# Down projection of a hybrid decoder layer: 18 of 22 contraction tiles in the seven-product block form

## The chip, the cores and the metric

The kernel runs on one core of a Trainium2 chip. The metric is device time in microseconds (us) for one launch, as the median of several runs. The engines go by their short names: PE is TensorE, DVE is VectorE, ACT is ScalarE, POOL is GpSimd, SP is SyncE, which issues nearly all DMA transfers of this kernel.

## The reference

One inference step of a decoder layer, for a prompt of 1024 tokens and 8 sample tokens, which share all weights: 1032 token columns in all. Two mixers (a gated linear recurrence and a state-space mixer) are followed by an output projection, and then by the part that matters here:

```python
x = x + jnp.concatenate([o_a, y], axis=-1) @ w['w_out']
h = rmsnorm(x, w['norm2_w'])
gate, val = jnp.split(h @ w['w_up'], 2, axis=-1)              # 1024 -> 2 x 2816
gate, buf_f_new = causal_dwconv(gate, buf_f, w['ffn_conv_w'], w['ffn_conv_b'])   # width 3
x = x + (jax.nn.silu(gate) * val) @ w['w_down']               # 2816 -> 1024
...
y = rmsnorm(x, final_norm_w)
```

All of it is float32. A matrix product is made of three passes over operands that are split into a high part (rounded to the fp32r format) and a low part (the rest): high×high, high×low, low×high.

## The kernel before

Data lie transposed: 128 features on the partitions, 1032 tokens along the free axis. `DFF` = 2816 makes 22 feature tiles (`FT`), the model width 1024 makes 8 (`KT`). The tokens are split into four blocks of 258 (`QW`).

**Up projection, seven-product form.** A step j makes one feature tile of the gate and one of the value for all tokens. Both are products of a 2×2 block problem: two output tiles (gate, value), two halves of the contraction (4 tiles each), two token blocks. Instead of eight block products it takes seven, p1 to p7, of sums and differences of the operands. The weight sums are made on POOL from two staged tiles `ws` (`up_load`), and split into high `wh` and low `wl` by ACT and DVE (`up_split`). The token operands (`usets`) are made once before the stage. A step runs the products in `ORDER` = p1, p6, p5, p7, p2, p4, p3, each for both halves of the tokens (i = 0, 1), 12 matmuls a product, 168 in all. The results of one product are folded into the others by methods named after the products: some on ACT (copies of p1 and p5), some on DVE (adds that read PSUM), two POOL subtractions after p7. p1, p7 and p3 use three PSUM banks in turn (`ua`), the others four (`ub`). `up_close` then runs the convolution (`fcv`, one ACT and two DVE operations over 1048 columns), SiLU on ACT, the product with the value on DVE, and stores the activation tile in device memory (`act_d`).

**What sets the order.** The PE order is written out by hand: the loops issue matmuls one by one, and other work is tied to them with `tick()` and `after(n, ...)` (do it n matmuls later) and `spread(pieces, n)` (a piece of a generator every n matmuls). The order of the other engines' queues comes from a scheduler of the framework, which keeps to dependences; each queue then runs strictly in order. The staging tile `ws` has two buffers; the load of the next weights waits on SP until DVE has made the last split that reads the old ones.

**Down projection.** Five rounds of four contraction tiles (`RND`), and then a last stage of two tiles. In a round the four activation tiles are loaded from `act_d` and split (`act_load`); for each pair of output tiles 512 KB of weights are loaded and split (`wload`), and `down` runs 12 matmuls for each of 8 output tiles and 4 token quarters. DVE adds the PSUM result to the residual tile `xT`. The last stage takes its two tiles with resident weights (`wd`), quarter by quarter, in the order 3, 0, 1, 2; behind each quarter the final norm and the stores of the output (`fin`, `ot`) follow.

Names of tiles that appear below: `ub`, `ua`, `dn` are PSUM results; `ws`, `wt` staged weights and their sums; `wh`, `wl` their high and low parts; `us` intermediate blocks of an up step; `wdh`, `wdl` the plain weights of the last stage; `ah`, `al` plain activations. Line 93 is the one place that issues a matmul.

Of the kernel before, what the change touches and what calls it, by code (L numbers as in the profile page):

```python
# [16 lines left out]
P = 128  # L17
# [16 lines left out]
RND = 4  # L34
NRES = 4
# [8 lines left out]
        "x5": (UW, 5), "us": (QW, 10), "t": (512, 4)}  # L44
# [6 lines left out]
def hybrid_layer(  # L51
# [1124 lines left out]

    def up_load(j):
        ws = []
        for c0 in (0, DFF):
# [4 lines left out]
            last_w[0] = SP.dma_start(t.rearrange("p (k m) -> p k m", m=P),  # L1184
                                     w_up[0, :, c0 + j * P:c0 + (j + 1) * P].rearrange("(k p) m -> p k m", p=P))
            ws.append(t)
        (g1, g2), (v1, v2) = ((t[:, :512], t[:, 512:]) for t in ws)
        sums = {}

        def add(name, x_, y_):  # L1190
            sums[name] = tl("t", "wt")
            G.tensor_tensor(sums[name], x_, y_, op=ALU.add)
            return sums[name]
# [8 lines left out]
    def up_split(j, n):  # L1202
# [4 lines left out]
        lo = pool.tile([P, KT * P], F32R, tag="wl", bufs=2, name=nm("wl"))  # L1207
        for i, name in enumerate(ORDER[2 * n:2 * n + 2]):
            cs = slice(i * 512, (i + 1) * 512)
# [4 lines left out]
    class Up:  # L1214

        def __init__(self, j, i, ext, val):
            self.j, self.i, self.ext, self.val = j, i, ext, val

        def mul(self, name):
            w, u = wparts[self.j][1][name], usets[self.i][name]  # L1220
            ps = (psmm.tile([P, 512], F32, tag="mm", name=nm("ua")) if name in ("p1", "p7", "p3") else bank("ub"))[:, :QW]
            for k in range(4):
                for n, (a, x) in enumerate(((w[0], u[0]), (w[0], u[1]), (w[1], u[0]))):
                    mm(ps, a[:, k, :], x[:, k, :], start=k == 0 and n == 0, stop=k == 3 and n == 2)
# [3 lines left out]
        def at(self, c):  # L1228
            return slice((2 * self.i + c) * QW, (2 * self.i + c + 1) * QW)

# [33 lines left out]

    def up_open(j):
# [16 lines left out]
    def ups(j, seq):  # L1282

        us_ = up_open(j)
        for n, (name, i) in enumerate(seq):
            yield from us_[i].mul(name)
            if n == 2 and j + 1 < FT:
                up_load(j + 1)
            if n in (5, 9, 13) and j + 1 < FT:
# [3 lines left out]
        up_close(j, us_[0])  # L1293

    with tc.manual_schedule(engines={mybir.EngineType.PE}):
# [18 lines left out]

        xT = [None] * KT
        quarters = [slice(0, 256), slice(256, 512), slice(512, 768), slice(768, NT)]

        def act_load(k):
            hi, lo = tl("hT", "ah", F32R), tl("hT", "al", F32R)
            SP.dma_start(lo.bitcast(F32), act_d[k])  # L1320
            split_in(hi, lo, slice(0, NT))
            return hi, lo
# [14 lines left out]

        after(200, lambda: spread(ffn_conv_states(), 60))

        def down(w, kt, msl, acts, c):  # L1340
            q = quarters[c]
            ps = psmm.tile([P, 512], F32, tag="mm", name=nm("dn"))[:, :q.stop - q.start]
            for k in range(kt):
                hi, lo = acts[k]
                wh, wl = w(k)
                mm(ps, wh[:, msl], hi[:, q], start=(k == 0), stop=False)
                mm(ps, wh[:, msl], lo[:, q], start=False, stop=False)
                mm(ps, wl[:, msl], hi[:, q], start=False, stop=(k == kt - 1))
                tick()
            return ps  # L1350

        acts = [act_load(k) for k in range(RND)]
        for r0 in range(0, FT - RND, RND):
            nk = min(RND, FT - r0)
            rows = slice(r0 * P, (r0 + nk) * P)
            nxt = [act_load(r0 + RND + k) for k in range(min(RND, FT - r0 - RND))]
            for m in range(0, KT, 2):
                wh, wl = wload(w_down[0, rows, m * P:(m + 2) * P], nk, 2 * P)
                for i in range(2):
                    if xT[m + i] is None:  # L1360
# [74 lines left out]
```

## Time and profile before

| what | value |
|---|---|
| median of 3 runs | 1800.01 us (1798.77 to 1801.22) |
| profiled execution, its time | 1797.69 us |
| its span, first to last instruction | 1795.8 us |
| granted TensorE clock, mean | 0.987 |
| busy: PE, DVE, ACT, POOL | 97%, 63%, 44%, 23% |
| DMA moved | 182.34 MB, mean 102 GB/s |

In the rows of the profile `L1211` is line 1211 of the kernel, `x44` counts instructions, `out<-in` names tiles with their buffer numbers left out. A row of the groups gives busy time and mean duration, and then the engine's idle time before these instructions with what ended it. A row of the stretches gives the stretch, its length, the busy time of PE, the weight loads, DVE, ACT and POOL in it with their instruction counts, the granted clock, the mean busy share of the 16 DMA engines and GB/s. A row of the timeline gives start, duration, engine, line and operation. A row of the chain of waits gives start, duration and what ran. A row of the waits gives who waited for whom, us in total, how often, and the longest.

### The profile page before, as it was taken

To read this page: it belongs to the slowest core of one execution; us is meant where nothing else is said; L and a number is where in the kernel's file an instruction comes from. 1 tells how busy PE (TensorE), PEld (TensorE's weight loads), DVE (VectorE), ACT (ScalarE), POOL (GpSimd) and SP (SyncE) were. 2 spreads that over 40 slices of the span, in tenths; PEclk is the share of its full clock that TensorE was granted. 3 is DMA by queue.
4 is the path that set the end of the run, shared out by engine and by line. 5 is a ranking of instruction groups with operands and counts; after the bars stand their busy time and mean duration, and the time that the engine had idled before them with its cause. 6 is when DMAs were issued, how large, how long until landed. Compare 5 with 4: busy or idle time off the path is not lost.

```text
span 1795.8 us, 38458 instructions
## 1 busy us (share of the span) xinstructions
PE 1735.7 (97%) x16143; PEld 1680.2 (94%) x16143; DVE 1126.4 (63%) x2011; ACT 792.8 (44%) x1416; POOL 409.5 (23%) x415
## 2 busy tenths in 40 slices
PE   7999899999999999999999988999999999999998
PEld 6998799998999999999899977999999999999997
DVE  6667966565554555557636779656666667555545
ACT  7677688353444344345323344333433334111114
POOL 2113322110110110111100454445444542000001
PEclk9999999999999999999999988999999999999999
DMA  4144634642221222234334431222222225422212
GB/s 153 39 125 135 193 96 124 186 132 97 73 78 50 84 74 73 62 96 148 93 123 130 138 95 45 94 75 72 76 85 89 72 71 201 149 89 96 96 60 95
DMA packets 218019, 182.34 MB, mean 102 GB/s; under 512 B 13388, under 2 KB 195158, under 8 KB 217830
## 3 DMA queue, kind: packets, MB, share of 16 engines
q1 hardware_dynamic: 217558, 179.80, 32.0%
q8 instruction: 126, 2.06, 0.5%
q14 instruction: 47, 0.39, 0.1%
q0 software_dynamic: 288, 0.10, 0.0%
HBM read 141.53 MB, written 38.52 MB: 100 GB/s over the span
## 4 chain that ended last, share of the span: by engine, by line
PE 78%; DVE 7%; DMA 5%; ACT 4%; issue 3%; POOL 2%; SPq 1%; DVEq 0%; POOLq 0%; ACTq 0%
PE mm L93 31%; PE ub L93 14%; PE dn L93 13%; PE ua L93 10%; PE a L93 2%; PE o L93 1%; DMA csb<-cs_d 1%; DMA Bb<-bc_d 1%; ACT csb L530 1%; PE kv L93 1%; DVE wl L184 1%; POOL Cb L631 1%; SPq L175 1%; DMA ml<-mix_d 1%; ACT L531 1%
## 5 line engine op out<-in xcount | busy, mean ns | idle before, releaser
L93 PE MATMUL mm<-hh,wh 128*128 128x344 f32 x1248 | 407.9, 327 | 0.0
L93 PE MATMUL mm<-hl,wh 128*128 128x344 f32 x1248 | 406.2, 326 | 0.0
L93 PE MATMUL mm<-hh,wl 128*128 128x344 f32 x1248 | 404.3, 324 | 0.0
L93 PEld LDWEIGHTS mm<-hh,wh 128*128 128x128 f32 x1248 | 236.2, 190 | 3.5 <-issue 0.9
L93 PEld LDWEIGHTS mm<-hl,wh 128*128 128x128 f32 x1248 | 236.1, 189 | 2.6 <-issue 0.9
L93 PEld LDWEIGHTS mm<-hh,wl 128*128 128x128 f32 x1248 | 236.4, 189 | 2.3 <-issue 1.0
L183 ACT CAST wh<-ws 128x1024 fp32r<-128x1024 f32 x96 | 100.5, 1047 | 259.5 <-PE dn L93 133.6
L93 PE MATMUL ub<-uh,wh 128*128 128x258 f32 x704 | 200.2, 284 | 7.8 <-ACT uh L1129 7.8
L93 PE MATMUL ub<-ul,wh 128*128 128x258 f32 x704 | 199.5, 283 | 0.8 <-DVE ul L1130 0.8
L93 PE MATMUL ub<-uh,wl 128*128 128x258 f32 x704 | 199.4, 283 | 0.0
L93 PE MATMUL dn<-ah,wh 128*128 128x256 f32 (+1 forms) x640 | 181.2, 283 | 1.2 <-DVE x L1365 1.2
L93 PE MATMUL dn<-al,wh 128*128 128x256 f32 (+1 forms) x640 | 180.6, 282 | 0.0
L93 PE MATMUL dn<-ah,wl 128*128 128x256 f32 (+1 forms) x640 | 180.1, 281 | 0.0
L93 PE MATMUL mm<-mh,wh 128*128 128x258 f32 x512 | 149.1, 291 | 10.7 <-DVE x L1026 10.7
L184 DVE TENSOR_TENSOR wl<-ws,wh 128x1024 fp32r<-128x1024 f32 x96 | 127.0, 1323 | 50.0 <-ACT wh L183 47.3
L93 PE MATMUL ua<-uh,wh 128*128 128x258 f32 x528 | 149.5, 283 | 0.0
L93 PE MATMUL ua<-ul,wh 128*128 128x258 f32 x528 | 149.1, 282 | 0.0
L93 PE MATMUL ua<-uh,wl 128*128 128x258 f32 x528 | 148.9, 282 | 0.0
L93 PE MATMUL mm<-ml,wh 128*128 128x258 f32 x512 | 147.7, 289 | 0.3 <-DVE ml L985 0.3
L93 PE MATMUL mm<-mh,wl 128*128 128x258 f32 x512 | 147.4, 288 | 0.0
L93 PEld LDWEIGHTS ub<-uh,wh 128*128 128x128 f32 x704 | 133.8, 190 | 8.1 <-ACT uh L1129 8.1
L93 PEld LDWEIGHTS ub<-ul,wh 128*128 128x128 f32 x704 | 134.3, 191 | 1.1 <-DVE ul L1130 1.1
(333 smaller groups left out, 3920.5 us busy)
## 6 DMA issues: line engine op xcount, KB each, us to landing
ws<-in_w_in_dram SPq DMA_DIRECT2D x52, 512.0 KB
ws<-in_w_up_dram SPq DMA_DIRECT2D x44, 512.0 KB
ws<-in_w_out_dram SPq DMA_DIRECT2D x24, 512.0 KB
act_d<-val SPq DMA_DIRECT2D x22, 516.0 KB
al<-act_d SPq DMA_DIRECT2D x22, 516.0 KB
ws<-in_w_down_dram SPq DMA_DIRECT2D x22, 512.0 KB
ml<-mix_d SPq DMA_DIRECT2D x48, 172.0 KB
csb<-cs_d SPq DMA_DIRECT2D x32, 256.0 KB
```

The source lines that it names most:

```text
L93: PE.matmul(out, lhsT, rhs, start=start, stop=stop)
L175: SP.dma_start(dst, src)
L183: A.copy(wh[:, :n], ws[:, :n])
L184: V.tensor_tensor(wl[:, :n], ws[:, :n], wh[:, :n].bitcast(F32), op=ALU.subtract)
L530: A.activation(csb3[:, h, :], csb3[:, h, :], AF.Relu, scale=-1.0, bias=cst[:, h0 + h:h0 + h + 1])
L531: A.activation(csb, csb, AF.Exp, scale=-1.0)
L631: G.tensor_tensor(Cb, Sd, Cb, op=ALU.mult)
```

## The change

Eighteen of the 22 contraction tiles of the down projection go into the seven-product form; four stay plain, in the last stage (`DPLAIN` = 4, two before). There are three rounds (`NRD`) of three pairs of contraction tiles (`RP`). A Down step j ≥ 22 belongs to round r and output pair q (`divmod(j - FT, 4)`), twelve steps in all, written (r,q) below. The 2×2 block problem is: two output tiles, two contraction tiles of a pair, two token blocks of 258; the three pairs of a round are summed in PSUM, so that a product takes 9 matmuls and a step 126.

The code of the up step is shared: `Seven.mul` runs a product, `Up` and `Down` differ in operands and in what happens to a result. In a Down step DVE adds p2, p4 and p3 straight to the residual tiles, with two further adds from SBUF for each half of the tokens, and POOL does four operations for each half.

The token operands of a pair need sums of two activation tiles, so they are made during the up projection, by `act_set`: after every odd step up to 17 it loads four blocks of the two finished activation tiles, makes four differences and sums on POOL, splits seven operands into high and low (`put`: ACT copy, DVE subtraction, 258 columns each), and stores them in device memory (`as_d`), for i = 0 and i = 1, one piece every 21 matmuls. In the down projection a round needs 21 tiles of 1032 columns (seven operands of three pairs, high and low of one half of the tokens side by side, both halves). They are loaded into buffers that the up projection leaves (`slot`); a list of loads (`wanted`) is worked off as buffers come free: the first round's during the last up step, the next round's first five during the step before the last of a round, the rest in the round's last step, each when a product is done. The loads and splits of the plain tiles (`last_tiles`) stand at the end of the same list.

```diff
-RND = 4
+RP, NRD = 3, 3
+DPLAIN = FT - 2 * RP * NRD
+    NSTEP = FT + 4 * NRD
     def up_load(j):
...
+            else:
+                r, q = divmod(j - FT, 4)
+                rows = w_down[0, 2 * RP * r * P:2 * RP * (r + 1) * P, (2 * q + i) * P:(2 * q + i + 1) * P]
+                for h2 in range(2):
+                    last_w[0] = SP.dma_start(t[:, h2 * n * P:(h2 + 1) * n * P].rearrange("p (k m) -> p k m", m=P),
+                                             rows.rearrange("(k two p) m -> two p k m", two=2, p=P)[h2])
...
+    class Down(Seven):
+        def operands(self, name):
+            return [[t[:, self.i, a, :] for t in dset[self.r, name]] for a in range(2)]
+        def p1(self, ps):
+            self.s = tl("us", "us")
+            A.copy(self.s, ps)
+        def p6(self, ps):
+            self.u2 = tl("us", "us")
+            V.tensor_tensor(self.u2, self.s, ps, op=ALU.add)
+        def p5(self, ps):
+            self.f = tl("us", "us")
+            A.copy(self.f, ps)
+            x_ = self.xg[:, self.at(0)]
+            G.tensor_tensor(x_, x_, self.s, op=ALU.add)
+        def p7(self, ps):
+            self.u3 = tl("us", "us")
+            V.tensor_tensor(self.u3, self.u2, ps, op=ALU.add)
+            G.tensor_tensor(self.u2, self.f, self.u2, op=ALU.subtract)
+            G.tensor_tensor(self.f, self.f, self.u3, op=ALU.subtract)
+            x_ = self.xv[:, self.at(1)]
+            G.tensor_tensor(x_, x_, self.f, op=ALU.add)
...
+        def p4(self, ps):
+            x_ = self.xg[:, self.at(1)]
+            V.tensor_tensor(x_, x_, ps, op=ALU.add)
+            V.tensor_tensor(x_, x_, self.u3, op=ALU.add)
...
+    def act_set(kp):
+        for i in range(2):
+            ab = tl("g", "ab")
+            for h2 in range(2):
+                SP.dma_start(ab[:, h2 * 2 * QW:(h2 + 1) * 2 * QW], act_d[2 * kp + h2][:, 2 * i * QW:2 * (i + 1) * QW])
+            yield
+            a1, b1, a2, b2 = (ab[:, n * QW:(n + 1) * QW] for n in range(4))
+            def put(name, src):
+                hl = tl("as", "as", F32R)
+                A.copy(hl[:, :QW], src)
+                V.tensor_tensor(hl[:, QW:], src, hl[:, :QW].bitcast(F32), op=ALU.subtract)
+                SP.dma_start(as_d[kp, ORDER.index(name)][:, 2 * i * QW:2 * (i + 1) * QW], hl.bitcast(F32))
+            put("p4", b2)
+            G.tensor_tensor(b2, b1, b2, op=ALU.subtract)
+            yield
+            put("p1", a1)
+            G.tensor_tensor(b1, a1, b1, op=ALU.subtract)
...
+    def wanted():
+        for r in range(NRD):
+            for name in ORDER:
+                for n in range(RP):
+                    while not free or r and turned[0] < (r - 1, 2):
+                        yield None
+                    yield lambda r=r, name=name, n=n: dset_load(r, name, n)
+        yield from last_tiles()
...
-        up_close(j, us_[0])
+            if i:
+                turn(j, name)
+        if j < FT:
+            up_close(j, us_[0])
+            if j % 2 and j < 2 * RP * NRD:
+                after(20, lambda: spread(act_set(j // 2), 21))
...
-        for r0 in range(0, FT - RND, RND):
...
+        for j in range(FT, NSTEP):
+            for _ in ups(j, [(name, i) for name in ORDER for i in range(2)]):
+                tick()
```

The PE order is unchanged up to the last up step. DVE's queue in the middle of an up step before: evictions of p7 (L1245), splits of two weights (L1211), evictions of p2 (L1251) and p4 (L1256).

```order
L1245 TENSOR_TENSOR us_17420<-us_17342,ua_17407 128x258
L1245 TENSOR_TENSOR us_17437<-us_17369,ua_17424 128x258
L1211 TENSOR_TENSOR wl_17470<-wt_17352,wh_17469 128x512
L1211 TENSOR_TENSOR wl_17470<-wt_17348,wh_17469 128x512
L1251 TENSOR_TENSOR fext_17291<-us_17308,ub_17441 128x258
L1251 TENSOR_TENSOR fext_17291<-us_17323,ub_17455 128x258
L1256 TENSOR_TENSOR fext_17291<-us_17420,ub_17475 128x258
L1256 TENSOR_TENSOR fext_17291<-us_17437,ub_17489 128x250
```

The same place now (p7 is L1265, the splits L1225, p2 L1271, p4 L1276; L1348 is the subtraction of `put`, from the block tile `ab`):

```order
L1265 TENSOR_TENSOR us_17743<-us_17650,ua_17725 128x258
L1265 TENSOR_TENSOR us_17760<-us_17682,ua_17747 128x258
L1225 TENSOR_TENSOR wl_17798<-wt_17660,wh_17797 128x512
L1348 TENSOR_TENSOR as_17670<-ab_17624,as_17670 128x258
L1348 TENSOR_TENSOR as_17702<-ab_17624,as_17702 128x258
L1271 TENSOR_TENSOR fext_17596<-us_17613,ub_17764 128x258
L1225 TENSOR_TENSOR wl_17798<-wt_17656,wh_17797 128x512
L1271 TENSOR_TENSOR fext_17596<-us_17631,ub_17783 128x258
L1276 TENSOR_TENSOR fext_17596<-us_17743,ub_17803 128x258
L1348 TENSOR_TENSOR as_17737<-ab_17624,as_17737 128x258
L1348 TENSOR_TENSOR as_17773<-ab_17624,as_17773 128x258
L1276 TENSOR_TENSOR fext_17596<-us_17760,ub_17821 128x250
```

Four of a step's seven new subtractions stand between the splits and the evictions of p2 and p4; the other three follow among the evictions of p3 and the convolution. POOL's queue over one up step before holds the four weight sums (L1192) and the four subtractions after p7 (L1246, L1247):

```order
L1192 TENSOR_TENSOR wt_17348<-ws_17346 128x512
L1192 TENSOR_TENSOR wt_17350<-wt_17348,ws_17344 128x512
L1192 TENSOR_TENSOR wt_17352<-ws_17344,ws_17346 128x512
L1192 TENSOR_TENSOR wt_17354<-wt_17350,ws_17344 128x512
L1246 TENSOR_TENSOR val_17292<-us_17384,us_17420 128x258
L1247 TENSOR_TENSOR us_17342<-us_17384,us_17342 128x258
L1246 TENSOR_TENSOR val_17292<-us_17399,us_17437 128x258
L1247 TENSOR_TENSOR us_17369<-us_17399,us_17369 128x258
L1267 MEMSET fext_17547 128x2
```

Now (sums L1205, the subtractions after p7 L1266 and L1267), the four block operations of `act_set` stand between them and the next step:

```order
L1205 TENSOR_TENSOR wt_17660<-ws_17652,ws_17654 128x512
L1205 TENSOR_TENSOR wt_17662<-wt_17658,ws_17652 128x512
L1266 TENSOR_TENSOR val_17597<-us_17697,us_17743 128x258
L1267 TENSOR_TENSOR us_17650<-us_17697,us_17650 128x258
L1266 TENSOR_TENSOR val_17597<-us_17717,us_17760 128x258
L1267 TENSOR_TENSOR us_17682<-us_17717,us_17682 128x258
L1352 TENSOR_TENSOR ab_17624<-ab_17624 128x258
L1355 TENSOR_TENSOR ab_17624<-ab_17624 128x258
L1358 TENSOR_TENSOR ab_17624<-ab_17624 128x258
L1361 TENSOR_TENSOR ab_17624<-ab_17624 128x258
L1431 MEMSET fext_17887 128x2
```

The weight sums of the next step come behind these operations. In the down projection, DVE's queue at the end of step (2,0), the third round's first (L1331 and L1332 are p3's adds to the residual, L980 the split of plain weights, L1225 the splits for step (2,1), L1304 the eviction of p6 in (2,1)):

```order
L1331 TENSOR_TENSOR x_2508_18612<-x_2508_18612,ua_20771 128x258
L1332 TENSOR_TENSOR x_2508_18612<-x_2508_18612,us_20643 128x258
L980 TENSOR_TENSOR wdl_20538<-ws_20539,wdh_20537 128x1024
L980 TENSOR_TENSOR wdl_20574<-ws_20575,wdh_20573 128x1024
L1225 TENSOR_TENSOR wl_20672<-ws_20619,wh_20671 128x384
L1225 TENSOR_TENSOR wl_20784<-ws_20619,wh_20783 128x384
L1225 TENSOR_TENSOR wl_20814<-ws_20622,wh_20813 128x384
L1225 TENSOR_TENSOR wl_20730<-wt_20625,wh_20729 128x384
L1225 TENSOR_TENSOR wl_20672<-wt_20627,wh_20671 128x384
L1225 TENSOR_TENSOR wl_20730<-wt_20629,wh_20729 128x384
L1225 TENSOR_TENSOR wl_20784<-wt_20631,wh_20783 128x384
L1304 TENSOR_TENSOR us_20827<-us_20799,ub_20817 128x258
```

All seven splits for (2,1) stand behind the last eviction of (2,0); in the steps (0,1) and (1,1) it is the same without the two plain splits, and in the other steps the splits stand among the evictions of the step before.

More of the change, by code (lines that the diff above doesn't have):

```diff
@@ L1265, in up_open @@
+    queue, turned = wanted(), [(-1, 0)]
     def up_open(j):
@@ L1338, in hybrid_layer @@
         after(200, lambda: spread(ffn_conv_states(), 60))
[L1340 to L1348, printed above, removed]
-                tick()
-            return ps
```

167 lines of the change are left out of this document (118 added, 49 removed).

## The prediction

> **What bounds the kernel now.** I read the page's busy shares first, then the chain of waits, then the stretches and the timeline of one tile of the up projection.
>
> ```profile
> PE 1735.7 (97%) x16143; PEld 1680.2 (94%) x16143; DVE 1126.4 (63%) x2011; ACT 792.8 (44%) x1416; POOL 409.5 (23%) x415
> 1278.53 5.78 PE ua L93 x48
> 1284.31 5.75 PE ub L93 x48
> 1530.17 66.05 PE dn L93 x552
> 1183.67:1485.57 301.90, 301.90 (x2523) 301.90 (x2522) 198.42 (x330) 116.57 (x211) 142.98 (x150) 1.00 0.25 80
> PE dn L93 <- DVE x L1365: 1.2, 2, 0.9
> ```
>
> TensorE is busy 97% of the span, and in both projections the chain is nothing but matmuls: 5.75/48 and 66.05/552 are both 0.1197 us for one product of about 258 columns. So one up tile (168 matmuls) takes 20.1 us, and the stretch over 15 tiles shows no idle PE: 301.9/15 = 20.13. In that stretch VectorE is busy 13.2 us of a tile, POOL 9.5, ACT 7.8; these three have room by their shares. Where up ends and down begins, PE loses only the 1.2 us of the last row. The kernel is a PE stream, so fewer matmuls are worth their full time as long as the stream is fed. Whether it still is, the timeline of a tile must tell:
>
> ```profile
> 1259.73 4.79 SPq L1184 DMA_DIRECT2D ws<-in_w_up_dram  x2
> 1263.45 0.68 DVE L1211 TENSOR_TENSOR wl<-ws,wh 128x512 fp32r<-128x512 f32 x1
> 1264.81 1.23 DVE L1279 TENSOR_TENSOR val<-val,fext 128x1032 f32<-128x1032 f32 x1 [0.68 <-ACT fext L1278]
> 1265.96 0.42 DVE L1237 TENSOR_TENSOR us<-us,ub 128x258 f32<-128x258 f32 x1
> 1268.07 1.37 POOL L1192 TENSOR_TENSOR wt<-ws 128x512 f32<-128x512 f32 x1 [10.55 <-DMA ws<-in_w_up_dram]
> 1270.76 1.30 POOL L1192 TENSOR_TENSOR wt<-ws,ws 128x512 f32<-128x512 f32 x1
> 1272.01 1.75 POOL L1192 TENSOR_TENSOR wt<-wt,ws 128x512 f32<-128x512 f32 x1
> 1271.49 1.12 DVE L1211 TENSOR_TENSOR wl<-wt,wh 128x512 fp32r<-128x512 f32 x1 [3.19 <-ACT wh L1210]
> 1272.53 0.74 DVE L1245 TENSOR_TENSOR us<-us,ua 128x258 f32<-128x258 f32 x2
> 1273.43 2.03 DVE L1211 TENSOR_TENSOR wl<-wt,wh 128x512 fp32r<-128x512 f32 x2 [0.15 <-ACT wh L1210]
> 1273.72 1.20 POOL L1246 TENSOR_TENSOR val<-us,us 128x258 f32<-128x258 f32 x1
> 1274.88 1.18 POOL L1247 TENSOR_TENSOR us<-us,us 128x258 f32<-128x258 f32 x1
> 1276.02 0.74 POOL L1246 TENSOR_TENSOR val<-us,us 128x258 f32<-128x258 f32 x1
> 1276.72 0.75 POOL L1247 TENSOR_TENSOR us<-us,us 128x258 f32<-128x258 f32 x1
> 1279.11 0.69 DVE L1211 TENSOR_TENSOR wl<-ws,wh 128x512 fp32r<-128x512 f32 x1
> 1279.71 0.68 DVE L1211 TENSOR_TENSOR wl<-wt,wh 128x512 fp32r<-128x512 f32 x1
> 1280.32 0.42 DVE L1263 TENSOR_TENSOR val<-us,ua 128x258 f32<-128x258 f32 x1
> 1280.79 1.31 DVE L334 SCALAR_TENSOR_TENSOR fcv<-fext,vcol,fcv 128x1048 f32<-128x1048 f32 x1
> 1282.02 0.42 DVE L1263 TENSOR_TENSOR val<-us,ua 128x258 f32<-128x258 f32 x1
> ```
>
> Alone, a 258-wide POOL add costs 0.70 (1276.02 to 1276.72) and a 512-wide VectorE subtraction 0.60 (1279.11 to 1279.71). Beside each other they take turns to the hundredth: the subtraction begun at 1271.49 waits until POOL's sum gives way at 1272.01 and ends 0.60 later, at 1272.61; that POOL sum then needs its own 1.25 (1270.76 to 1272.01 for the one before) and ends at 1273.76; two adds and two subtractions fill 1273.43 to 1276.06, 2.63 us, against 2×0.70 + 2×0.60 = 2.60 one after another. A VectorE operation that reads PSUM beside one SBUF input (0.74 for two at 1272.53, 0.42 alone) is not held up. So VectorE operations with two SBUF inputs and POOL operations have one turn between them.
>
> **The change part by part: PE.**
>
> ```profile
> L93 PE MATMUL dn<-ah,wh 128*128 128x256 f32 (+1 forms) x640 | 181.2, 283 | 1.2 <-DVE x L1365 1.2
> L93 PE MATMUL dn<-ah,wdh 128*128 128x256 f32 (+1 forms) x64 | 18.3, 286 | 0.0
> ```
>
> Down is now 3×(640+64) = 2112 matmuls. After: 12 steps × 14 products × 9 = 1512, and 4 plain tiles give 384: 216 fewer, 216 × 0.1197 = **-25.8**. The 1.2 us at the junction go (**-1.2**), since the first products no longer need the last activations.
>
> **Token sets in the up projection.** In tiles 2 to 19 each tile gains, on average, 7 casts on ACT, 7 subtractions of 258 on VectorE, 4 POOL adds of 258, and 9 transfers on SP (7 stores of 264 KB, 2 loads). ACT goes from 7.8 to some 10.7 us of 20.1 (0.42 for each cast, VectorE's time for 258 columns, an estimate): no bound. The transfers add 2.4 MB a tile, 119 GB/s to the 80 of the stretch's row: no bound either. The common turn of VectorE and POOL is one. Today, per tile: VectorE 7 splits × 0.60 + 2 convolution steps × 1.23 (1280.79 to 1282.02) + the product 1.15 (1264.81 to 1265.96) = 7.8; POOL 4 sums × 1.25 + 4 adds × 0.70 + 0.15 = 7.95; together 15.7 of 20.1. Added: 7 × 0.35 (258 columns on the line through 0.60 at 512 and 1.15 at 1032, an estimate from these rows) + 4 × 0.70 = 5.25, giving **20.95**, more than PE needs. That is the lower bound of a tile's length, reached only if the turn never stands idle.
>
> It does. The subtraction of the seventh weight (p3) frees the staging tile, whose reload leads to POOL's sums, and VectorE's split of p6 waits for the second of them. In the trace that loop runs from 1263.45 + 0.68 = 1264.13 to 1272.61: 8.5 us. From the p6 split to the next p3 split the queue orders hold, in turn: one sum and eight adds (1.25 + 8×0.70 = 6.85), five splits (3.0), six of the seven new subtractions (2.1), two convolution steps (2.46), two evictions that find no POOL work to hide behind (0.7): 15.1. Together 23.6, the upper bound. Between 20.95 and 23.6 I take **22.8**, near the upper end since the loop is measured: in the 8.5 us the last new subtraction, the product and one split have their place already, and going through two tiles turn by turn gave 22.7 to 23.1. Per tile +2.67; 18 tiles +48; about 2 us of it lie in the banks' slack at a tile's end (p3's first eviction, at 1280.32 in the trace, is wanted when the fourth product of the quoted four starts, 1278.53 + 3/4 × 5.78 = 1282.87): **+46** (from +13 to +60). Who waits: the p3 evictions stand behind the splits on VectorE, and the second p1 product of the next tile needs their bank.
>
> [...]
>
> **Down: the junctions.**
>
> ```profile
> 1518.00:1520.00 2.00, 2.00 (x19) 2.00 (x18) 2.00 (x4) 0.25 (x2) 1.88 (x2) 1.00 1.03 403
> 1520.00:1522.00 2.00, 2.00 (x19) 2.00 (x18) 2.00 (x6) 1.21 (x2) 0.00 (x0) 1.00 0.99 405
> 1522.00:1524.00 2.00, 2.00 (x18) 2.00 (x17) 2.00 (x3) 2.00 (x3) 0.00 (x0) 1.00 1.04 417
> 1524.00:1526.00 2.00, 2.00 (x19) 2.00 (x18) 2.00 (x4) 0.99 (x2) 0.00 (x0) 1.00 1.02 384
> L979 DVE TENSOR_TENSOR wdl<-ws,wdh x2: 1224/1224/1225, 1728.3 to 1733.8; 128x1024 fp32r<-128x1024 f32 x2
> ```
>
> With all engines of the queue busy (share 1.0) 402 GB/s move, so a tile of 528 KB takes 1.31 us, and a round's 21 token-set tiles 27.6 us against a step's 15.1 us of PE.
>
> *Up to round 0.* Set loads start some 2 us into the last up tile, T. Before the weights of the second step can land, the queue carries 21 set tiles, 2 activation stores and 4 residual tiles (27 × 1.31 = 35.4) and 2.6 us of weights: with 1.4 us of latency T+41.4, split by T+42.2. PE would be there at T + 20.1 + 15.1 = T+35.2. Stall 7.0, and 1.1 more for p6, behind two POOL sums: **8** (6 to 12).
>
> *Round 0 to 1.* Here 16 tiles (21 us) load over the last step and the first of the round, and each comes before its product. But VectorE's order has the splits for step (1,1) behind all evictions of (1,0): two evictions (0.84) and one split (0.55), then p6's cast on ACT behind an eviction: **2** (1 to 5).
>
> *Round 1 to 2.* In front of the same splits stand two 1.22 us splits of plain weights, and these hold both staging tiles: 0.84 + 1.22, then a reload of about 3.3 us (3.94 from 1264.13 to 1268.07 for 512 KB; here 393), cast and split 1.05 give 6.4, then p6 +1: **7.3** (5 to 11). *Plain tiles:* 0.5 (0 to 4); their loads and splits lie beside the last step.
>
> [...]
>
> **Steps between.** POOL 8 × 0.70 + 4 × 0.97, VectorE 4 × 0.35 + 7 × 0.48 (384 columns, between the rows' sizes) make 14.2 of a step's 15.07: the same loop leaves steps of about 15.9. Eight plain steps, some slack in each round: **+4** (0 to 9).
>
> Sum: -25.8 - 1.2 + 46 + 8 + 2 + 7.3 + 0.5 + 4 = **+41**. Made against the profiled execution (span 1795.8, time 1797.69, 2.3 under the median of 1800.01) that is 1838.5 for such an execution; on the median, **1841**.
>
> **The rivals.**
> *The turn packs well.* If order and slack let POOL and VectorE alternate with no idle time, a tile takes 20.95: +13 in place of +46, sum +8, 1808. For it: PE's queue stalls let other work catch up. Against: the 8.5 us loop is a chain of dependences, not of queue places.
> *PE stays the bound, and the kernel is faster.* If the added 258-wide operations take the turn for no more than 4.4 us a tile (0.29 and 0.58 each instead of 0.35 and 0.70), the demand stays under 20.13, and if the new work falls into VectorE's idle 6 us, up loses nothing: the sum is -25.8 - 1.2 + 17.8 + 1 = -8, 1792. Against it stand the 2.63 us of four operations in turn.
> *SP holds back.* Its queue is in order: a weight load now stands behind stores that wait for VectorE, and two buffers of sets make ACT wait for a store to land. If each tile lost another 2 us, up would cost +82: 1877.
>
> **How the numbers follow.** Forecast 0.57 (own range 1825 to 1862), good packing 0.24 (1800 to 1825), PE-bound 0.10, SP 0.09. Leaving out the PE-bound case and most of the SP case gives 1802 to 1866. About 0.2% is what can be told from no change here: faster 0.09, same 0.05, slower 0.86.
>
> **What would show it.** Up tiles 2 to 19 of 22 to 23.5 us with PE idle before p1 products, released by VectorE's p3 eviction; 0.70 adds on POOL stretched well over 1 us; tiles 0, 1, 20 and 21 at 20.1; PE idle of 5 to 9 us in the first and the third round's second step and about 2 in the second's. I am wrong if up tiles stay at 20.1 us (then the turn was not the limit), or if the stalls sit before weight loads on SP.

## The result, and the profile after

The changed kernel takes **1858.4 us** (median of 4 runs, 1850.0 to 1860.3) against 1799.4 (4 runs, 1797.2 to 1801.2) on the same chip: ratio 1.0319, 95% interval 1.0284 to 1.0355. The forecast was 1841, with 1802 to 1866 as its range: slower, as foreseen, by 59 us where 41 were written down. The profiled execution has a span of 1858.5 against 1795.8, so the traces have **62.7 us** to explain. It was one of the longer of the four.

The page's first part, and then the stretch of the up projection from 1150 to 1550 us in before and in after (columns: window, length, busy time and instruction count of PE, weight load, VectorE, ScalarE, POOL, then the granted clock, the share of the DMA engines, GB/s):

```profile
PE 1742.6 (94%) x15927; PEld 1678.2 (90%) x15927; DVE 1228.6 (66%) x2193; ACT 851.7 (46%) x1638; POOL 618.7 (33%) x631
```
```profile
1150.00:1550.00 400.00, 398.81 (x3328) 398.39 (x3327) 265.23 (x437) 154.31 (x267) 173.04 (x183) 1.00 0.30 100
```
```profile
1150.00:1550.00 400.00, 371.37 (x2974) 367.80 (x2973) 305.75 (x509) 174.49 (x368) 237.88 (x245) 0.97 0.52 175
```

216 matmuls are gone from PE (16143 to 15927), and PE is no longer full: in the same 400 us it issues 2974 instead of 3328. No engine has taken its place by busy share; VectorE stands at 76%. Where PE stands still, its waits from 1050 us on say (engine, tile, line, what it waited for; total, times, longest; two rows at the start of up, which before has too, and the rows under 2 us are left out):

```profile
PE ua L94 <- DVE val L1283: 29.2, 18, 4.3
PE ua L94 <- ACT wh L1224: 8.9, 2, 5.4
PE ua L94 <- DVE x L1331: 5.6, 4, 3.3
PE ub L94 <- DVE wl L1225: 3.6, 3, 2.3
PE ua L94 <- DVE wl L1225: 2.2, 1, 2.2
```

The first row is the up projection: PE wants the bank that VectorE's p3 eviction (L1283) has not emptied, about once a tile. The others lie in the down steps. How long up takes is read from PE's first and last matmul in it, in before and in after:

```profile
1066.48 0.28 PE L93 MATMUL ua<-uh,wh 128*128 128x258 f32 x1
1522.65 0.28 PE L93 MATMUL ua<-uh,wl 128*128 128x258 f32 x1
```
```profile
1071.89 0.28 PE L94 MATMUL ua<-uh,wh 128*128 128x258 f32 x1
1572.65 0.28 PE L94 MATMUL ua<-uh,wl 128*128 128x258 f32 x1
```

Up has become **44.6 us** longer (500.8 for 456.2; forecast: +46), and what follows it **12.7** (forecast: -5). The other 5.4 us lie ahead of up, in code that both kernels share. They are scatter of the execution: in the traces of this document up starts anywhere between 1066.5 and 1075.5 us.

The loop that the prediction measured stands there again, in VectorE's, SP's and POOL's timelines of one tile of after:

```profile
1312.14 0.69 DVE L1225 TENSOR_TENSOR wl<-ws,wh 128x512 fp32r<-128x512 f32 x1
1314.57 0.43 DVE L1348 TENSOR_TENSOR as<-ab,as 128x258 fp32r<-128x258 f32 x1 [1.74 <-ACT as L1347]
1315.90 1.23 DVE L1443 TENSOR_TENSOR val<-val,fext 128x1032 f32<-128x1032 f32 x1 [0.90 <-ACT fext L1442]
1317.72 1.12 DVE L1225 TENSOR_TENSOR wl<-ws,wh 128x512 fp32r<-128x512 f32 x1
1320.67 1.11 DVE L1225 TENSOR_TENSOR wl<-wt,wh 128x512 fp32r<-128x512 f32 x1 [1.83 <-ACT wh L1224]
1321.71 0.74 DVE L1265 TENSOR_TENSOR us<-us,ua 128x258 f32<-128x258 f32 x2
```
```profile
1312.86 0.38 SPq L1191 DMA_DIRECT2D ws<-in_w_up_dram  x1
```
```profile
1316.76 1.53 POOL L1205 TENSOR_TENSOR wt<-ws 128x512 f32<-128x512 f32 x1 [8.26 <-DMA ws<-in_w_up_dram]
1318.38 1.61 POOL L1205 TENSOR_TENSOR wt<-wt,ws 128x512 f32<-128x512 f32 x1
```

The split of p3 ends at 1312.83, the reload is issued at 1312.86 and has landed by 1316.76, POOL's second sum ends at 1319.99, the split of p6 starts at 1320.67 and ends at 1321.78: 8.95 us, forecast 8.5. The evictions of p7 (L1265) stand behind it.

**What was not foreseen is in PE's own rows.** PE's timeline around one such wait, and the stretches there:

```profile
1305.89 0.28 PE L94 MATMUL ua<-uh,wl 128*128 128x258 f32 x1
1309.17 0.39 PE L94 MATMUL ua<-uh,wh 128*128 128x258 f32 x1 [3.00 <-DVE val L1283]
...
1310.46 0.42 PE L94 MATMUL ua<-uh,wh 128*128 128x258 f32 x1
1310.68 0.42 PE L94 MATMUL ua<-ul,wh 128*128 128x258 f32 x1
...
1313.67 0.29 PE L94 MATMUL ub<-uh,wh 128*128 128x258 f32 x1
1313.80 0.28 PE L94 MATMUL ub<-ul,wh 128*128 128x258 f32 x1
```
```profile
1310.00:1312.00 2.00, 2.00 (x13) 2.00 (x12) 2.00 (x4) 0.00 (x0) 0.00 (x0) 0.56 0.87 296
1312.00:1314.00 2.00, 2.00 (x12) 2.00 (x12) 0.83 (x2) 0.00 (x0) 0.00 (x0) 0.59 0.17 58
1314.00:1316.00 2.00, 2.00 (x19) 2.00 (x18) 0.53 (x2) 1.87 (x5) 0.00 (x0) 1.00 0.92 275
1310.50:1313.50 3.00, 3.00 (x16) 3.00 (x16) 2.33 (x4) 0.00 (x0) 0.00 (x0) 0.50 0.48 167
```

A wait of 3.00 us, one microsecond at full pace, and then 3.4 us in which a matmul starts every 0.215 us instead of every 0.12; the granted clock is 0.56 to 0.59, and 0.50 in the three microseconds that lie wholly inside (last row). Sixteen such steps hold about 1.5 us more than at the full pace. All steps between matmul starts can be sorted in this way: over 0.3 us a wait, 0.18 to 0.3 us the slow pace, each less the usual 0.12. In up after's waits hold 44.0 us and its slow steps 12.0, against 11.5 and 1.7 in before, which lie in before's first tile; behind up it is 31.2 and 9.3 against 2.4 and 1.3. So 32.5 us of waiting and 10.3 at the slow pace are new in up, 28.8 and 8.0 behind it: **18.3 us** more at the slow pace in all.

Only behind up are they clearly a price of their own: there four steps without a wait take 15.05 to 15.13 us, what PE needs for 126 matmuls at 0.12, so that PE sets the pace between the stalls. In up another engine sets the length of a tile, and slow steps can fall into time in which PE would have waited. Of the pairs of tiles from 3 to 18 in after and in two runs below whose up projection is after's (one set, direct plain), 18 hold slow steps and last 45.3 us on average, 6 hold none and last 45.0, with a spread of 0.6. That the slow pace lengthens up is not shown.

### The profile page after: what moved, and what is told of

It is laid out like the page before. It is cut to its first block, busy times and chain, and to the rows that moved or that the text cites. A ratio compares the mean times of both kernels' runs of the same rounds, so it can differ in the third digit from the quotient of the medians.

```text
span 1858.5 us, 39428 instructions
## 1 busy us (share of the span) xinstructions
PE 1742.6 (94%) x15927; PEld 1678.2 (90%) x15927; DVE 1228.6 (66%) x2193; ACT 851.7 (46%) x1638; POOL 618.7 (33%) x631
## 4 chain that ended last, share of the span: by engine, by line
PE 51%; DMA 13%; DVE 13%; issue 9%; POOL 8%; ACT 4%; SPq 1%; DVEq 0%; POOLq 0%; ACTq 0%
PE mm L94 32%; PE ub L94 4%; PE ua L94 3%; POOL wt L1205 3%; DMA ab<-act_d 3%; PE a L94 2%; PE dn L94 2%; DMA as_d<-as 2%; DMA ws<-in_w_down_dram 2%; DVE wl L1225 2%; DMA as<-as_d 2%; PE o L94 1%; POOL val L1266 1%; POOL us L1267 1%; DVE fcv L335 1%
## 5 line engine op out<-in xcount | busy, mean ns | idle before, releaser
L1225 DVE TENSOR_TENSOR wl<-wt,wh 128x512 fp32r<-128x512 f32 (+1 forms) x136 | 131.2, 977 | 108.9 <-ACT wh L1224 108.7
L94 PE MATMUL ua<-uh,wh 128*128 128x258 f32 x528 | 154.2, 292 | 28.9 <-DVE val L1283 28.7
L94 PE MATMUL mm<-mh,wh 128*128 128x258 f32 x512 | 148.6, 290 | 11.1 <-DVE x L1027 10.8
L970 POOL TENSOR_TENSOR sg<-sg,sq 128x512 f32<-128x512 f32 x16 | 24.2, 1532 | 381.9 <-DVE sq L641 239.9
L184 ACT CAST wh<-ws 128x1024 fp32r<-128x1024 f32 x76 | 79.6, 1047 | 127.6 <-PE mm L94 121.2
L1224 ACT CAST wh<-wt 128x512 fp32r<-128x512 f32 (+1 forms) x136 | 77.0, 580 | 128.7 <-POOL wt L1205 121.7
L94 PEld LDWEIGHTS ub<-uh,wl 128*128 128x128 f32 x704 | 135.4, 192 | 0.1
```

What stands on the lines that cost most here:

```text
L94: PE.matmul(out, lhsT, rhs, start=start, stop=stop)
L184: A.copy(wh[:, :n], ws[:, :n])
L970: G.tensor_tensor(oh, oh, sq[hf], op=ALU.mult)
L1224: A.copy(hi[:, cs], sums[name])
L1225: V.tensor_tensor(lo[:, cs], sums[name], hi[:, cs].bitcast(F32), op=ALU.subtract)
```

## Experiments

Theory A: the up projection pays for the ScalarE, VectorE and POOL work of `act_set`, not for its transfers. Rival C: it pays for transfers and SP's queue. Each run was timed in three rounds beside before, whose median in these comparisons was 1797.9 to 1800.0. "Up tile" is the mean from tile 2's first p3 eviction to tile 19's, "up" goes from PE's first matmul of the up projection to its last, and "rest" from there to the end of the span, all in the profiled execution. Runs with after's up projection differ by 3 us in "up".

| kernel | time, us | ratio (95%) | up tile, 2 to 19 | up | rest |
|---|---|---|---|---|---|
| before | 1799.4 | | 20.1 | 456.2 | 273.1 |
| after | 1858.4 | 1.032 (1.028-1.036) | 22.7 | 500.8 | 285.8 |
| transfers only | 1812.5 | 1.007 (1.005-1.008) | 20.4 | 459.2 | 283.9 |
| sets alone | 1843.2 | 1.024 (1.021-1.027) | 22.8 | 502.5 | 273.3 |
| adds on VectorE | 1868.1 | 1.037 (1.033-1.041) | 23.2 | 510.9 | 284.9 |
| no adds | 1840.8 | 1.022 (1.020-1.025) | 21.9 | 487.2 | 283.5 |
| late splits | 1855.6 | 1.031 (1.029-1.033) | 22.6 | 499.9 | 285.5 |
| regrouped splits | 1840.4 | 1.022 (1.020-1.025) | 22.3 | 493.0 | 274.5 |
| one set | 1842.4 | 1.024 (1.022-1.026) | 22.7 | 503.7 | 268.6 |
| direct plain | 1852.8 | 1.030 (1.027-1.032) | 22.7 | 500.6 | 279.3 |
| reordered | 1846.6 | 1.025 (1.022-1.028) | 23.1 | 506.1 | 270.2 |
| reordered, direct | 1844.3 | 1.025 (1.023-1.026) | 22.9 | 504.1 | 269.7 |
| reordered, no store | 1861.9 | 1.033 (1.030-1.036) | 23.7 | 522.0 | 269.7 |
| regrouped, prefetch, direct | 1844.5 | 1.025 (1.021-1.028) | 22.9 | 500.9 | 272.0 |

### Work or transfers

Transfers only: `act_set` loads its blocks and stores them raw, with no ScalarE, VectorE or POOL work; the down steps multiply by raw blocks.

```diff
-            put("p4", b2)
-            G.tensor_tensor(b2, b1, b2, op=ALU.subtract)
...
+            def put(name, n):
+                SP.dma_start(as_d[kp, ORDER.index(name)][:, 2 * i * QW:2 * (i + 1) * QW], ab[:, n * 2 * QW:(n + 1) * 2 * QW])
+
+            for k, name in enumerate(("p4", "p1", "p2", "p5", "p7", "p6", "p3")):
+                put(name, k % 2)
```

> The changed kernel, but act_set only moves data: it loads the activation blocks and stores them unchanged as token sets; its 7 ACT casts, 7 VectorE subtractions and 4 POOL adds per up tile are left out (so the down projection multiplies other data). Theory A (VectorE and POOL take turns): the turn's demand falls back to 15.7 us a tile, up tiles take 20.13 us, and the whole is some 50 us shorter, about 1808. Theory B (transfers and SP's in-order queue hold the tiles up): up tiles stay near 22.7 us, about 1855.

Sets alone: before, with `act_set` added to its up projection; the sets are made and not used.

```diff
+        if j % 2 and j < 18:
+            after(20, lambda: spread(act_set(j // 2), 21))
```

> The kernel before, with the token sets made during the up projection and stored, and never used: the plain down projection stays. Theory A: up tiles 2 to 19 take 22.7 us as in the changed kernel, about +48 on the kernel before, 1848. Theory B the same. Rival C (the up tiles are late because of what the last up step and the down steps ask of the queues): no change, 1800.

The two split the change cleanly. Without the work 46 us go, and PE's wait for the p3 eviction falls from 29.2 to 2.5; with the sets alone before loses 43 us, all of it in up (456.2 to 502.5; the rest is as in before). PE's waits in the two:

```profile
PE ua L94 <- DVE val L1283: 2.5, 4, 1.2
```
```profile
PE ua L93 <- DVE val L1263: 29.6, 15, 4.2
```

So theory A holds and SP's queue is out: moving 126 stores and 36 loads costs up 3 us. It also gives the new down projection by itself: transfers only is 12.5 us slower than before by the medians; by the profiles it is 14.0, of which 10.7 lie behind up.

What transfers only cannot show is what the engines lose by waiting for the sets' transfers, since in it no engine waits for them. In after ScalarE does, between 1150 and 1550 us, for a place in the two `as` buffers:

```profile
ACT as L1347 <- DMA as_d<-as: 79.0, 43, 4.6
```

In the same stretch the chain of waits, followed back from the end, runs for 11.1% through the loads of `ab`, which has one buffer, and for 8.8% through these stores. Two runs below take one of these waits away each, but change VectorE's order with it; more buffers were not tried.

### Which part of the work

```diff
-            G.tensor_tensor(b2, b1, b2, op=ALU.subtract)
+            V.tensor_tensor(b2, b1, b2, op=ALU.subtract)
```

(and so for the four adds); in the other kernel the four adds are left out, so that plain blocks stand in place of four of the seven operands.

> The changed kernel with the four adds of act_set on VectorE instead of POOL. Theory A, demand alone: the turn is asked for 4 x 0.35 instead of 4 x 0.70 us a tile, 19.55 in all, under PE's 20.13: up tiles 20.1, about 1810. Theory A with the loop (reload of the staged weights, sums, split of p6): the loop loses only the difference, 22.7 - 1.4 = 21.3 us a tile, 1833. Theory B: no change, 1858, or more, as VectorE is busier.

> The changed kernel with the four adds of act_set left out (the sets are then the plain blocks, so the down projection multiplies other data); casts, subtractions and transfers stay. Demand alone: 18.15 us a tile, up tiles at 20.13, 1810. With the loop: 22.7 - 2.8 = 19.9, so also PE's 20.13 or slightly over, 1810 to 1815. If the seven subtractions rather than the adds were what counts, tiles stay above 21.5, 1838 or more. Theory B: 1855.

Both went against the demand of the turn. The prediction's lower bound (20.95 us, what VectorE and POOL hold in turn) falls in both kernels, and with the adds on VectorE the tile still became longer, 23.2; without them it lost 0.8 of its 2.6 us, as the third case of that expectation had it (tiles above 21.5: the seven subtractions count more than the adds). No run leaves out the VectorE subtractions alone, or the ScalarE copies. What VectorE does in the 400 us, in before, after and with the adds on VectorE (busy, mean ns; idle before, and what ended it):

```profile
L1211 DVE TENSOR_TENSOR wl<-wt,wh 128x512 fp32r<-128x512 f32 x72 | 69.5, 984 | 61.5 <-ACT wh L1210 61.5
```
```profile
L1348 DVE TENSOR_TENSOR as<-ab,as 128x258 fp32r<-128x258 f32 x120 | 76.8, 660 | 16.5 <-ACT as L1347 16.4
L1225 DVE TENSOR_TENSOR wl<-wt,wh 128x512 fp32r<-128x512 f32 x71 | 75.0, 1067 | 67.4 <-ACT wh L1224 67.4
```
```profile
L1348 DVE TENSOR_TENSOR as<-ab,as 128x258 fp32r<-128x258 f32 x119 | 67.3, 581 | 10.1 <-ACT as L1347 9.9
L1225 DVE TENSOR_TENSOR wl<-wt,wh 128x512 fp32r<-128x512 f32 x68 | 61.8, 909 | 62.8 <-ACT wh L1224 62.8
```

Before already waits 61.5 us at the p6 split, 3 us a tile, and it costs nothing, since VectorE afterwards waits for PE. VectorE's waits for PE in the same 400 us, in before and in after:

```profile
DVE fext L1256 <- PE ub L93: 34.6, 35, 1.0
DVE us L1237 <- PE ub L93: 12.9, 17, 0.8
DVE x L1365 <- PE dn L93: 7.3, 8, 1.0
```
```profile
DVE us L1257 <- PE ub L94: 1.7, 2, 0.9
```

The third row of before lies in its down projection, which starts at 1523 us. Up itself had 34.6 + 12.9 = 47.5 us of room in 373, and 1.7 in 400 are left: work and waits for other engines together have gone from (373 - 47.5)/373 of 20.13, 17.6 us a tile, to nearly all of the tile. The sets put 4.4 us of splits a tile and their own waits behind a wait that stayed. An add moved to VectorE lengthens that queue too.

### Shortening the loop

Late splits calls the three weight splits three products later; regrouped splits lets p2 and p3 be split together, so that both staging tiles are free two products sooner.

```diff
-            if n in (5, 9, 13) and j + 1 < NSTEP:
-                up_split(j + 1, (5, 9, 13).index(n))
+            if n in (8, 11, 13) and j + 1 < NSTEP:
+                up_split(j + 1, (8, 11, 13).index(n))
```

> The three weight splits of the next tile are called three places later (after products 8, 11 and 13 of 14 instead of 5, 9 and 13), in the up projection and in the down steps alike; the work is the same. Theory A' (what lengthened the up tiles is the order of VectorE's queue: the split of p6, called after product 5, waits for POOL's sums, which wait for the reload after p3's split, and the PSUM evictions queued behind it are held): a place is 1.44 us, so the split gets 4.3 us more and is no longer late (it came 9.0 us after p3's split where 4 places give 5.8); up tile 22.7 falls to 20.2-21.2, the wait of PE for the eviction val falls from 29 us to under 12, time 1815-1835. Theory B (the sum of VectorE's and POOL's work with the sets fills the tile, wherever it is called): up tile 22.4-23.0, time 1852-1862. Theory C (the loop is set by the reload alone, so that what is called later comes later at its other end too, the next p3 split being pushed out): tile 22.7-24, time 1858-1880.

```diff
+    GROUPS = ("p1", "p6"), ("p5", "p7"), ("p2", "p3"), ("p4",)
-        for i, name in enumerate(ORDER[2 * n:2 * n + 2]):
+        for i, name in enumerate(GROUPS[n]):
```

> The last two splits change places: p2 and p3 are split after product 13, p4 (a sum in its own tile) in the next tile after product 1. So both staging tiles are free after product 13 and the next reload can start about 2 places, 2.9 us, earlier; the work is the same. Theory A': p6's split, which came 9.0 us after the freeing split, is late by 3.2 us (4 places are 5.8); 2.9 us of that goes, up tile 22.7 falls to 20.4-21.6, time 1818-1842. Theory B (sum of VectorE's and POOL's work): up tile 22.4-23.0, time 1852-1862. Between: the extra split after product 13 delays the evictions there, tile 21.6-22.4.

Late splits tested nothing: only PE's order is written by hand, and the scheduler put VectorE's split back where it was (the wait there is 67.1 us, 67.4 in after; the 3 us less are within the runs' spread). Regrouping did move it:

```profile
L1349 DVE TENSOR_TENSOR as<-ab,as 128x258 fp32r<-128x258 f32 x119 | 77.0, 663 | 30.6 <-ACT as L1348 30.6
L1226 DVE TENSOR_TENSOR wl<-wt,wh 128x512 fp32r<-128x512 f32 x72 | 70.3, 986 | 31.2 <-ACT wh L1225 30.9
```

The wait halves, from 67.4 to 30.9; but the sets' own wait doubles, and only 0.4 us of a tile is won (22.1, which later expectations quote, came from fewer tiles). 18 us are gained in all; by the profiles 7.8 in up and 11.3 behind it. So the time lies in the range of theory A', but the tile does not (22.3 is in the range between the theories): more than half was gained where theory A' did not look. The reordered kernel takes the first split's wait away altogether; its p6 results also move from the four banks `ub` to the three `ua`:

```diff
-    ORDER = ("p1", "p6", "p5", "p7", "p2", "p4", "p3")
+    ORDER = ("p1", "p2", "p6", "p5", "p7", "p4", "p3")
+    GROUPS = ("p1", "p2"), ("p6", "p5"), ("p7", "p3"), ("p4",)
...
-            ps = (psmm.tile([P, 512], F32, tag="mm", name=nm("ua")) if name in ("p1", "p7", "p3") else bank("ub"))[:, :QW]
+            ps = (psmm.tile([P, 512], F32, tag="mm", name=nm("ua")) if name in ("p1", "p6", "p7", "p3") else bank("ub"))[:, :QW]
```

> The seven products are taken in the order p1 p2 p6 p5 p7 p4 p3 and the next tile's weights are split in the groups p1+p2, p6+p5, p7+p3, p4: the first split needs no sum of POOL's, and both staging tiles are free after product 13 as in the regrouped kernel. The work is the same. In the trace of the late splits VectorE's order had not changed (its scheduler put the p6 split back right behind the p6 evictions, 67.1 us of waiting as before), so this is the test that kernel was meant to be. Theory A' (VectorE stands at a split that waits for reload and sums, with PSUM evictions queued behind it): regrouping took its wait from 67.4 to 30.9 us in 400 us and the tile from 22.7 to 22.1, here it falls under 15 us and the tile to 20.3-21.3; up saves 28-48 us, the steps' first products come sooner too (ACT wh wait 8.9 us shrinks): time 1805-1828. Theory B (the sum of VectorE's and POOL's work with both locked out by each other): the tile stays 21.8-22.4, time 1838-1850.

```profile
DVE as L1349 <- ACT as L1348: 66.8, 50, 5.1
DVE wl L1226 <- ACT wh L1225: 0.7, 1, 0.7
```

It did, 0.7 us are left, and the tile is no shorter, 23.1, above the ranges of both theories: the same 67 us now stand at the sets' splits. A wait took the place of the one removed; what the other use of the banks did to the tile was not tried by itself. The stores behind that new wait were left out next (126 stores; the down steps load raw rows instead):

```diff
-                SP.dma_start(as_d[kp, ORDER.index(name)][:, ...], hl.bitcast(F32))
```

> The reordered kernel without the sets' stores: the 126 stores of finished blocks are left out, and the down steps load as many raw rows of the activations in place of the sets. Splits, sums and the loads of ab are all still made. In the reordered kernel VectorE no longer waits for the weights' split (0.7 us in 400 us instead of 67.4) but waits 66.8 us for the sets' rounding copy on ScalarE, which waits 64.7 us for the load of ab and 64.6 us for its own stores (two buffers). Theory Q (VectorE's queue is in order and full: what lengthens a tile is any wait that stands in it, whichever is last): without the stores about half of those waits go, tile 22.9 to 21.2-22.0, time 1812-1832. Theory B (the work under the mutual lock fills the tile): tile 22.4-23, time 1838-1848.

This was slower than with them, 23.7 a tile, long and short tiles in turn (about 25 and 22.5). The scheduler now puts seven of the sets' splits in every tile, where the reordered kernel has six and eight in turn, ScalarE waits for POOL's differences (59.1 us for the first of them), and VectorE waits for PE again (18.9 us). Both theories missed it, and it doesn't price the stores.

The last try, on the regrouped kernel, loads each block of `ab` by itself as soon as its place is free, and the plain rows directly:

```diff
-                SP.dma_start(ab[:, h2 * 2 * QW:(h2 + 1) * 2 * QW], act_d[2 * kp + h2][:, ...])
+                if i == 0 and name in ("p5", "p7", "p6", "p3"):
+                    load(1, n)
```

> The regrouped kernel with two more edits and the same result: the plain rows loaded straight into place, and the four blocks of ab loaded one by one, those of the second half as soon as the first half has used up their places (and the whole chain begun 2.4 us later after a tile's end, when its rows have landed). Theory Q: the regrouped kernel's two waits in VectorE's queue were 30.9 us for the weights' split and 30.6 us for the sets' copy in 400 us; the second falls by half or more, tile 22.1 to 21.0-21.6, and the plain rows give 5: time 1813-1828. Theory B: tile 21.9-22.3, time 1833-1838. Neither is under before's 1800.

Theory Q missed: 1844.5, no better than regrouped splits alone, with 22.9 us a tile. ScalarE hardly waits for `ab` any more (4.8 us in the 400), but the wait for the weights' split is back at 53.3 us, and ScalarE's waits for its own stores stay (73.4).

### The down projection

One set: rounds 1 and 2 multiply by round 0's sets, and the 42 loads of the later sets are left out.

```diff
-        return [[t[:, self.i, a, :] for t in dset[self.r, name]] for a in range(2)]
+        return [[t[:, self.i, a, :] for t in dset[0, name]] for a in range(2)]
```

> Rounds 1 and 2 multiply by round 0's token sets: the 42 loads of the later sets (22 MB) are left out, and the plain tiles' loads start in step (2,0) as before the edit. The up projection is unchanged (22.7 a tile). If the loads price the junctions between rounds, the waits of 2.2+2.3 us at (1,1), 3.3 us at (2,0) and the slow clock after them go, and (2,1)'s 5.4 us stays in part because it hangs on the plain tiles' weights: time 1843-1852. If the junctions are set by the weights' own chain (reload, sums, splits) and not by the sets' loads: 1855-1860. From this the clock can be read too: with no stalls over 2 us in rounds 1 and 2 the granted clock there should stay at 1.00.

Direct plain: the plain weight rows no longer pass through the two staging tiles of the steps' weights.

```diff
-            ws = wpool.tile([P, KT * P], F32, tag="ws", bufs=2, name=nm("ws"))
-            SP.dma_start(ws, w_down[0, ...])
-            split(ws, hi[:, :DM], lo[:, :DM])
+            SP.dma_start(lo[:, :DM].bitcast(F32), wd_d[k])
+            split_in(hi, lo, slice(0, DM))
```

> The weight rows of the four plain tiles are copied once into an own DRAM buffer early on and then loaded straight into the place of the lo half, as the activations' are, not through the two staging tiles that the steps' weights use. Theory: step (2,1) lost 5.4 us because its two staging tiles stood behind the plain rows' splits; that wait and part of the slow clock after it go: time 1850-1855. Rival: the weights of (2,1) land late anyway, since the DMA queues are full of the sets' loads: 1856-1860.

The same edit on the reordered kernel:

> The reordered kernel with the plain tiles' weight rows loaded straight into place (5.6 us less by itself). If the two do not overlap: 4-6 us under the reordered kernel. If the reordering has already taken step (2,1)'s wait: within 2 us of it. Against before: theory A' says it ends 0-25 us over before's 1800, since the down projection keeps its junctions (+11 less 6) and the up tile still holds 0.2-1 us more than 20.13.

The set loads are worth 16 us (median), the plain rows' staging 5.6, which is less than the runs of either kernel spread (the profiles' rests differ by 6.5); at (2,1) direct plain leaves a wait of 3.6 us of 5.4. On the reordered kernel, whose own rest was already 15.6 us shorter, the direct rows give 2.3, within the spread of the runs. Stretches of after and of one set over the down steps show what the loads did:

```profile
1574.00:1849.00 275.00, 248.63 (x1968) 243.32 (x1968) 167.20 (x318) 79.96 (x180) 143.45 (x147) 0.96 0.49 177
```
```profile
1571.50:1831.00 259.50, 245.65 (x1985) 241.12 (x1983) 162.62 (x319) 78.98 (x181) 142.44 (x147) 0.98 0.31 103
```

Behind up, PE's waits go from 31.2 to 17.1 us by the steps between its rows, and the time lost to the slow pace from 9.3 to 6.3. The clock did not stay at 1.00 as that expectation had it: a wait of 5.3 us at (2,1) is left.

No kernel beat before. Free set work (transfers only) would still leave 12.5 us of loss, and the best version that does all the work, regrouped splits, still loses 42.

## Why the prediction was right, and where it was wrong

- **216 matmuls, -25.8; up/down junction, -1.2**: PE's matmuls fell by 216, and no wait of PE stands where up ends.
- **Token sets, +46**: up grew by 44.6 in after and by 46.4 in sets alone, at the place named (PE before a p1 product, waiting for VectorE's p3 eviction), with 22.7 a tile for 22.8. The lower bound was not broken, but the runs refuted that the tile follows the demand of the turn (adds on VectorE: less demand, a longer tile). The convolution steps that the turn's sum counts in met no POOL work in up (1.30 us each, in before and in after); ahead of up before's trace shows such steps held up beside POOL (last section). The loop was right in its length, but as the cause it is half the story: shortening it helped a little, and taking its wait away moved the wait. Shown is that the ScalarE, VectorE and POOL work of the sets costs this time, and that VectorE's queue is then full of work and waits. Not shown is which of these waits could be packed better, those for the sets' own loads and stores included; the tries that did all the work left the tile between 22.3 and 23.2.
- **A sign that did not show**: POOL's adds were to be stretched well over 1 us. The four new ones took 0.81 to 1.07 us on average in the same 400 us, and the old ones 0.95 and 0.97, where before has 0.95 and 0.98.
- **Inside the +46**: it was worked out as the length of a tile, and that came. On PE it is made of 32.5 us of waiting and 10.3 at the slow clock, which no step of the prediction had.
- **Up to round 0, +8**: about 6 (3.45 for the split, and five waits of about 0.6 for sets). The 1.4 us of latency in the forecast are an estimate near what before's trace shows for one load: issued on SP at 1264.16, and by stretches of 0.25 us its data come at 10 and 43 GB/s from 1265.00 and at 233 from 1265.50 on. **Round 0 to 1, +2**: 4.6. **Round 1 to 2, +7.3**: 8.7, 3.3 of them a step early: at (2,0) PE waits for p3's eviction at L1331, since the weights were issued behind the set loads. At (2,1) 5.4 us came about as worked out; direct plain, which takes the plain rows out of the staging tiles, leaves 3.6 of them, so that the staging tiles are a part of it and not all. **Steps between, +4**: the seven steps without a junction lost 3.3 in all, four of them next to nothing. **Plain tiles, +0.5**: 1.4.
- **The step that failed is the sum of down**: -5.2 was forecast, +12.7 measured. The waits were forecast at 21.8 with the steps between, and 28.8 more than before's came; 8.0 more are matmuls at the slow pace behind them (0.215 us for 0.12). The forecast priced a stall at its own length.
- **The total**: 1858.4 lies in the range, near its top, because the range was wide. Up was right to 1.4 us; the down steps missed by 18, and by the profiles 5.4 are scatter ahead of up.
- **Rivals**: "the turn packs well", "PE stays the bound" and "SP holds back" are refuted as forecasts: up tiles are 22.7, neither 20.95 nor 20.13 nor 24.8, and moving the data costs 3 us in all of up. The last rival's second half, ScalarE waiting for a store to land, did come (79.0 us in 400); what it costs is open.

## What to carry to other kernels

Ask of the engine that empties the banks not how busy it is but how much of its time is work plus waits for others; when its waits for the bound engine are all but gone, it is the first suspect, here at 76% busy and with 1.7 us of such waits in 400. Where PE sets the pace, price a stall of two microseconds or more above its length: behind up the slow stretches after such stalls held 1.5 to 2.5 us more than the same matmuls at full pace. Where another engine does, as in up, an extra price was not shown. Compare stages from their own first instruction on, since an execution can enter a stage several microseconds late (5.4 here). And before an experiment on an order, look whether the order of that engine changed at all: a wait taken out of a full queue can come back at the next entry (67.4 us at the weights' split in after, 66.8 at the sets' in the reordered kernel).

## What the hardware showed beyond that

- In the up projections of after, regrouped and reordered, from the second tile on, 18 of 26 waits of 1.76 to 4.26 us were followed by 2.8 to 4.5 us at the slow pace (0.215 us for 258 columns; in after at a granted clock of 0.50), and none of 27 shorter ones was. A wait of 1.76 us was enough in the reordered kernel, and one of 2.46 in after was not.
- The common turn of VectorE and POOL shows with long operations too. In before's trace, ahead of up, a convolution step of 1056 columns takes 1.30 us alone and 1.90 when it starts while POOL is at work; it ends 1.12 after POOL's operation:

```profile
199.66 2.06 POOL L568 TENSOR_TENSOR S<-S,etot 128x512 f32<-128x512 f32 x1
200.94 1.90 DVE L334 SCALAR_TENSOR_TENSOR xbc<-ext,vcol,xbc 128x1056 f32<-128x1056 f32 x1
203.36 1.30 DVE L334 SCALAR_TENSOR_TENSOR xbc<-ext,vcol,xbc 128x1056 f32<-128x1056 f32 x1
```

- The product of 1032 columns takes 1231 ns in after and 2322 in the reordered kernel. That it stands beside POOL's sums there is the author's estimate; no row here shows it:

```profile
L1443 DVE TENSOR_TENSOR val<-val,fext 128x1032 f32<-128x1032 f32 x18 | 22.2, 1231 | 8.3 <-ACT fext L1442 8.3
```
```profile
L1444 DVE TENSOR_TENSOR val<-val,fext 128x1032 f32<-128x1032 f32 x18 | 41.8, 2322 | 0.0
```
